# Where the operands of the down-projection pieces stand in ScalarE's queue, in both feed-forwards of a fused encoder block

## The chip, the core and the metric

The kernel runs on one core of a Trainium2 chip. A core has five engines with a queue each: TensorE (PE in the profile, its weight loads PEld), VectorE (DVE), ScalarE (ACT), GpSimd (POOL) and SyncE (SP). SP and POOL only issue DMAs here. An engine takes its instructions in the order of its queue. The metric is device time in microseconds (us), the median of several runs.

## The reference

One layer of a streaming encoder on 256 tokens of width 2048, all in float32:

```python
def swiglu(h, w_up, w_down):
    gate, up = jnp.split(h @ w_up, 2, axis=-1)
    return (jax.nn.silu(gate) * up) @ w_down

x = x + 0.5 * swiglu(rms_norm(x, ffn1_norm), ffn1_w_up, ffn1_w_down)
...   # gated recurrences (HGRN2 and RG-LRU), then cross-attention: "the middle" below
x = x + 0.5 * swiglu(rms_norm(x, ffn2_norm), ffn2_w_up, ffn2_w_down)
return rms_norm(x, final_norm)
```

Only the two feed-forwards are touched. Their hidden width is 5632, so `w_up` is 2048 x 11264 and `w_down` 5632 x 2048.

## The kernel before

**Precision.** Float32 operands are split in two: a high part `h`, rounded to the matmul's input type, and a low part `l = raw - h`. A product a·b is made of three matmuls: a_h·b_h, a_l·b_h (lines L547, L548) and a_h·b_l (L550). `split` makes both parts of a weight tile: ACT writes `h` (L138), then DVE writes `l` (L139).

**Pieces.** Weights come in pieces of 128 x 2048 (1 MB) that are loaded (`raw`), split and used once. `plan` lists all pieces in the order of their use; `weights` keeps two of them prepared ahead, by calling `prepare`. There are three kinds that matter here:

- *fast* up pieces: the matrix product of a 2x2 block with seven block products in place of eight. Beside the weights (512 columns by 4, of which 3 are split as `h`, `l`, 1536 columns) they need four sums of them, `td`, 2048 columns. In the first feed-forward (ffn1) DVE makes the sums, L285 the first two, L287 and L288 one each; in the second (ffn2) some come ready from DRAM (loaded at L277; they were made during the middle). The sums are split in two halves of 1024 columns into `th` and `tl`: the last four lines of `prepare`. The second half (called the *second high part* below) needs L287 and L288, and PE uses it last.
- *plain* down pieces: one load (L270), one `split` of 2048 columns.
- *added* down pieces: ACT writes `l = -raw` (L254), a POOL DMA adds the weights to that from DRAM (L255), and ACT writes `h` later (L263). Their load is L253.

**Groups.** The hidden width is worked off in 11 groups of 512. From the fourth group on a group is eight up pieces (seven or eight of them fast), then four down pieces of earlier groups, here D1, D2, D3 and D4 in the order of use. D1, D2 and D3 are plain, D4 is added. D1 follows the last fast piece of its group. While the down pieces run, the group's seven sums in PSUM are turned into gate and up: L634 on ACT, L635, L636, L643, L646 on DVE, the SiLU at L580 on ACT (twice) and the product at L581 on DVE (twice). Transposes on PE (L588) and `hidop` (L592, L593) follow, and D4's products after the transposes. L662 adds a finished down result to the residual. In ffn1 these values are named `ev`, in ffn2 `hid` and `hd`.

**What sets the order.** A scheduler orders each engine's queue by its own estimate of times; only data dependences, buffers and hints bind it. Such a hint is `tc.issue_after(ins)`: every instruction traced inside is queued behind `ins` on the engine of `ins`; it adds no wait by itself. Buffers that matter: three `raw`, three `h`, three `l`; ffn2 has two `raw2` tiles more. A `raw` tile is free for its next load when the last split that reads it has run.

Of the kernel before, what the change touches and what calls it, by code (L numbers as in the profile page):

```python
# [77 lines left out]
def block_kernel(ctx: ExitStack, tc: tile.TileContext, xT, xin, memT, vec, gfin, bgate, lruw, wu1, wd1, win, wv,  # L78
# [55 lines left out]
    done = {}  # L134


    def split(h, l, raw):
        done["high"] = act.activation(h, raw, ACT.Copy).ins  # L138
        done["low"] = dve.tensor_tensor(out=l, in0=raw, in1=h.bitcast(F32), op=ALU.subtract).ins  # L139

    def split_tiles():
        return hp.tile([P, 2048], F32R, name="h", tag="h"), lp.tile([P, 2048], F32R, name="l", tag="l")


    plan, ahead, made_ahead = [], [], []
# [60 lines left out]
    def beside(i):  # L206

        if under_way and (i >= under_way[0][0] or "prep" not in scoped):
            next(under_way.pop(0)[1])
        if made_ahead and "prep" in scoped and i >= turn[0] and i < first_second - 4:  # L210
            turn[0] = i + (3 + len(made_ahead) % 2 if "scores" in scoped else 3 if len(made_ahead) % 3 else 2)
            steps = make_ahead(*made_ahead.pop(0))
            next(steps)
            under_way.append((i + (2 if "scores" in scoped else 3), steps))
# [5 lines left out]
    def weights(*key):  # L220
        while plan and len(ahead) < 2:
            i = next(planned)
            k, src, kind = plan.pop(0)
            if i == 0:
                in_turn.enter_context(tc.manual_schedule(engines={sp.engine, act.engine, dve.engine}))
            if i < len(head):
                head[i]()
            if plan and plan[0][2] == "added":
                begun.append(begin_added(plan[0][1]))
            ahead.append((k, prepare(src, kind, 4 if i < 4 else 1)))  # L230
            if i in rest:
                rest[i]()
            beside(i)
            if i == 7:
                in_turn.close()
        k, w = ahead.pop(0)
        assert k == key, (k, key)
        return w
# [4 lines left out]
    def raw_tile():  # L243

        if "raw2" in scoped and next(loads) % 5 > 2:
            return scoped["raw2"].tile([P, 2048], F32, name="raw2", tag="raw2")
        return rawp.tile([P, 2048], F32, name="raw", tag="raw")

    def begin_added(src):

        raw = raw_tile()
        l = lp.tile([P, 2048], F32R, name="l", tag="l")
        sp.dma_start(raw, src)  # L253
        act.activation(l, raw, ACT.Copy, scale=-1.0)  # L254
        nc.gpsimd.dma_start(l, src, accum_op=ALU.add)  # L255
        return raw, l

    def prepare(src, kind, cuts=1):

        if kind == "added":  # L260
            raw, l = begun.pop(0)
            h = hp.tile([P, 2048], F32R, name="h", tag="h")
            done["high"] = act.activation(h, raw, ACT.Copy).ins  # L263
            return h, l
        raw = raw_tile()
        n = 2048 // cuts
        if kind == "plain":
            h, l = split_tiles()
            for a in range(0, 2048, n):
                sp.dma_start(raw[:, a:a + n], src[:, a:a + n])  # L270
                split(h[:, a:a + n], l[:, a:a + n], raw[:, a:a + n])
            return h, l
        if kind == "ready":
            src, t = src
            sp.dma_start(raw[:, 512:], src[:, 512:])
            td = raw_tile()
            sp.dma_start(td, t)  # L277
        else:
            sp.dma_start(raw, src)
            if "raw2" in scoped:  # L280
                td = raw_tile()
            else:
                td = scoped["wide"].tile([P, 2048], F32, name="td", tag="wide")
            two = [v[:, a:a + 1024].rearrange("p (i n) -> p i n", i=2) for v, a in ((td, 0), (raw, 512))]
            dve.tensor_tensor(out=two[0], in0=raw[:, None, :512].broadcast_to([P, 2, 512]), in1=two[1],  # L285
                              op=ALU.subtract)
            dve.tensor_tensor(out=td[:, 1024:1536], in0=raw[:, 1024:1536], in1=td[:, :512], op=ALU.subtract)  # L287
            dve.tensor_tensor(out=td[:, 1536:], in0=raw[:, 1536:], in1=td[:, 1024:1536], op=ALU.subtract)  # L288
        h, l = split_tiles()
        if kind != "fast added":  # L290
            split(h[:, 512:], l[:, 512:], raw[:, 512:])
        else:
            act.activation(l[:, 512:], raw[:, 512:], ACT.Copy, scale=-1.0)
            nc.gpsimd.dma_start(l[:, 512:], src[:, 512:], accum_op=ALU.add)
            done["high"] = act.activation(h[:, 512:], raw[:, 512:], ACT.Copy).ins
        th = hp.tile([P, 2048], F32R, name="h", tag="h")
        if "wide" in scoped:
            tl = scoped["wide"].tile([P, 2048], F32R, name="tl", tag="wide")
        else:
            tl = lp.tile([P, 2048], F32R, name="tl", tag="l")  # L300
        for a in (0, 1024):
            split(th[:, a:a + 1024], tl[:, a:a + 1024], td[:, a:a + 1024])
        return (h, l), (th, tl)

    def product(xs, *ws, late=()):
# [19 lines left out]
    def two_ahead(xs, name, i, at, late=()):  # L325

        if i == at:
            both = product(xs, weights(name, i), weights(name, i + 1), late=late)
            two_ahead.next = both[1]
            return both[0]  # L330
        return two_ahead.next if i == at + 1 else product(xs, weights(name, i))[0]
# [233 lines left out]
    def ffn(name, pairs, sq, then, begin=(), sums=()):  # L565
# [37 lines left out]

        for at, e in enumerate(order):
            w = weights(name, *e)
            kind = e[0]
            following = order[at + 1][0] if at + 1 < len(order) else None
# [708 lines left out]
```

## Time and profile before

| | |
|---|---|
| median of 3 runs | 2424.43 us (2424.29, 2424.43, 2427.4) |
| the profiled execution | 2427.28 us, of which the span from first to last instruction is 2425.5 us |
| mean granted TensorE clock | 0.998 |
| engines busy | PE 99%, DVE 84%, ACT 60%, POOL 4% |
| feed-forwards | ffn1 from the start to about 702 us; ffn2 from about 1739 us to the end |

In a row of the timeline stand the start, the duration, the engine, the line, the operation, what it writes and reads, and how many instructions are merged; in brackets the idle time of that engine ahead of it and what ended it. A matmul over 512 columns has a duration of 0.39 us in such rows, but they are pipelined: four in a row take 1.07 us, so one starts every 0.227 us.

### The profile page before, as it was taken

What the parts mean: (1) busy time and instruction counts of PE and PEld (TensorE: products, weight loads), DVE (VectorE), ACT (ScalarE), POOL (GpSimd) and SP (SyncE); (2) the same over time, 40 slices, a digit from 0 to 9 for tenths busy, and PEclk for the clock granted to TensorE, in tenths of its full rate; (3) what the DMA queues carried; (4) which work ended last, traced back from release to release, by engine and by line L of the source; (5) the groups of instructions that cost most, each with busy time, mean ns of one, the idle gap of its engine ahead of it and who ended that gap; (6) DMA issues with size and microseconds to landing.
All of it is one profiled execution on the core that took longest, in us unless ns stands there. A gap on an engine that the chain in (4) does not pass through costs nothing.

```text
span 2425.5 us, 30763 instructions
## 1 busy us (share of the span) xinstructions
PE 2409.3 (99%) x12139; PEld 2013.6 (83%) x12139; DVE 2025.6 (84%) x2260; ACT 1455.0 (60%) x1485; POOL 102.2 (4%) x166
## 2 busy tenths in 40 slices
PE   9999999999999999999999999999999999999998
PEld 8888888888788888888888888888888788888887
DVE  7999999998876868779776788777789999999995
ACT  8567677777664454476434555445676666666664
POOL 0000000000000000000000000000000000000000
PEclk9999999999999999999999999999999999999999
DMA  7579999988858776778989889977798878787873
GB/s 294 195 229 287 272 272 270 275 269 268 266 183 323 268 289 241 294 289 323 346 313 349 310 332 354 335 272 263 264 343 308 285 266 293 273 286 276 294 273 144
DMA packets 102385, 684.31 MB, mean 282 GB/s; under 512 B 11361, under 2 KB 11617, under 8 KB 29281
## 3 DMA queue, kind: packets, MB, share of 16 engines
q1 hardware_dynamic: 78192, 518.68, 57.5%
q0 software_dynamic: 23328, 162.54, 22.4%
q8 instruction: 95, 1.56, 0.2%
q10 hardware_dynamic: 720, 1.13, 0.1%
q14 instruction: 50, 0.40, 0.0%
HBM read 619.39 MB, written 62.91 MB: 281 GB/s over the span
## 4 chain that ended last, share of the span: by engine, by line
PE 91%; DVE 3%; DMA 3%; ACT 1%; issue 1%; ACTq 0%; DVEq 0%; SPq 0%
PE acc L547 16%; PE acc L548 16%; PE acc L550 16%; PE acc L313 11%; PE acc L338 8%; PE acc L341 8%; PE acc L339 8%; PE acc L316 6%; DMA raw<-wd 2%; DVE tl L139 1%; ACT h L138 1%; DVE l L139 1%; PE acc L588 1%; PE acc L477 1%; DMA t<-prep 0%
## 5 line engine op out<-in xcount | busy, mean ns | idle before, releaser
L138 ACT ACTIVATE h<-raw 128x2048 fp32r<-128x2048 f32 (+3 forms) x578 | 870.5, 1531 | 620.2 <-PE acc L339 189.6
L139 DVE TENSOR_TENSOR l<-raw,h 128x2048 fp32r<-128x2048 f32 (+2 forms) x406 | 837.3, 2065 | 187.6 <-ACT h L138 186.1
L547 PE MATMUL acc<-h,xh 128*128 128x512 f32 x1241 | 485.2, 392 | 2.7 <-ACT h L138 2.4
L548 PE MATMUL acc<-h,xl 128*128 128x512 f32 x1241 | 483.0, 390 | 0.0
L338 PE MATMUL acc<-h,ops 128*128 128x512 f32 x832 | 326.8, 393 | 0.0
L339 PE MATMUL acc<-h,ops 128*128 128x512 f32 x832 | 324.5, 390 | 0.0
L547 PEld LDWEIGHTS acc<-h,xh 128*128 128x128 f32 x1241 | 233.3, 188 | 56.2 <-ACT h L138 8.0
L547 PE MATMUL acc<-h,hidop 128*128 128x512 f32 x704 | 276.5, 393 | 2.3 <-ACT h L138 2.2
L313 PE MATMUL acc<-ops,h 128*128 128x512 f32 x1152 | 278.2, 393 | 0.0
L548 PE MATMUL acc<-h,hidop 128*128 128x512 f32 x704 | 274.8, 390 | 0.0
L548 PEld LDWEIGHTS acc<-h,xl 128*128 128x128 f32 x1241 | 233.3, 188 | 47.5
L313 PEld LDWEIGHTS acc<-ops,h 128*128 128x128 f32 x1152 | 211.7, 188 | 41.6
L139 DVE TENSOR_TENSOR tl<-raw,h 128x1024 fp32r<-128x1024 f32 x172 | 203.7, 1220 | 14.9 <-ACT h L138 14.5
L341 PE MATMUL acc<-l,ops 128*128 128x512 f32 x832 | 205.8, 389 | 0.0
L550 PE MATMUL acc<-l,hidop 128*128 128x512 f32 x704 | 189.3, 389 | 0.0
L138 ACT ACTIVATE h<-td 128x1024 fp32r<-128x1024 f32 x126 | 131.3, 1057 | 92.9 <-PE acc L548 42.3
L341 PEld LDWEIGHTS acc<-l,ops 128*128 128x128 f32 x832 | 156.2, 188 | 32.4
L338 PEld LDWEIGHTS acc<-h,ops 128*128 128x128 f32 x832 | 156.2, 188 | 32.2
L339 PEld LDWEIGHTS acc<-h,ops 128*128 128x128 f32 x832 | 156.3, 188 | 31.5
L139 DVE TENSOR_TENSOR tl<-td,h 128x1024 fp32r<-128x1024 f32 x126 | 152.0, 1220 | 31.2 <-ACT h L138 31.0
L200 DVE TENSOR_TENSOR prep<-prep 128x512 f32<-128x512 f32 x232 | 159.7, 689 | 20.9 <-DMA prep<-wu 17.1
L550 PE MATMUL acc<-l,xh 128*128 128x512 f32 x645 | 176.4, 389 | 0.0
(242 smaller groups left out, 2739.4 us busy)
## 6 DMA issues: line engine op xcount, KB each, us to landing
raw<-wu SPq DMA_DIRECT2D x114, 1024.0 KB, 6.3
raw<-wd SPq DMA_DIRECT2D x88, 1024.0 KB, 6.3
prep<-wu POOLq DMA_DIRECT2D x58, 1024.0 KB, 7.8
t<-prep POOLq DMA_DIRECT2D x58, 1024.0 KB, 7.8
raw<-t SPq DMA_DIRECT2D x58, 1024.0 KB, 6.9
raw<-wu SPq DMA_DIRECT2D x58, 768.0 KB, 5.0
raw<-win SPq DMA_DIRECT2D x40, 1024.0 KB, 4.8
raw<-wg SPq DMA_DIRECT2D x32, 1024.0 KB, 6.1
```

What stands on the lines that cost most here:

```text
L138: done["high"] = act.activation(h, raw, ACT.Copy).ins
L139: done["low"] = dve.tensor_tensor(out=l, in0=raw, in1=h.bitcast(F32), op=ALU.subtract).ins
L200: dve.tensor_tensor(out=b[o], in0=b[x], in1=b[y], op=ALU.subtract)
L313: pe.matmul(acc, h[:, k * P:(k + 1) * P], xs[k], start=k == 0, stop=False)
L316: done["product"] = pe.matmul(acc[:, :T], l[:, k * P:(k + 1) * P], xs[k][:, :T], start=False, stop=k == KT - 1).ins
L338: pe.matmul(accs[t], x[:, t * P:][:, :P], h[j], start=first and j == 0, stop=False)
L339: pe.matmul(accs[t], x[:, T + t * P:][:, :P], h[j], start=False, stop=False)
L341: done["product"] = pe.matmul(accs[t], x[:, t * P:][:, :P], l[j], start=False, stop=last and j == 3).ins
L477: pe.transpose(acc[:, z * T + t * P:][:, :P], tile[:, t * 512 + (2 * y + z) * P:][:, :P], ident)
L547: pe.matmul(acc, ah, bh, start=start, stop=False)
L548: pe.matmul(acc, al, bh, start=False, stop=False)
L550: pe.matmul(acc, ah, bl, start=False, stop=stop)
```

## The change

`prepare` learns whether a piece is a down piece. The two operations of a plain down piece's split are traced inside `issue_after(done["sums"])`, where `done["sums"]` is the last ACT instruction of the sums of the latest fast piece: its second high part. So ACT's write of a plain down piece's `h` is queued behind the second high part of the fast piece in front. Added pieces return earlier and are not touched, nor is any DMA's line. For D2 and D3 the same `ins` holds.

```diff
-            ahead.append((k, prepare(src, kind, 4 if i < 4 else 1)))
+            ahead.append((k, prepare(src, kind, 4 if i < 4 else 1, k[1] == "down")))
...
-    def prepare(src, kind, cuts=1):
+    def prepare(src, kind, cuts=1, down=False):
...
                 sp.dma_start(raw[:, a:a + n], src[:, a:a + n])
-                split(h[:, a:a + n], l[:, a:a + n], raw[:, a:a + n])
+                with tc.issue_after(done["sums"]) if down else ExitStack():
+                    split(h[:, a:a + n], l[:, a:a + n], raw[:, a:a + n])
...
         for a in (0, 1024):
             split(th[:, a:a + 1024], tl[:, a:a + 1024], td[:, a:a + 1024])
+        done["sums"] = done["high"]
```

The lines below the first edit in `prepare` move by one or two: L285 becomes L286, L634 becomes L636; L254 and L263 keep their numbers. The text names lines by their numbers before. What the scheduler makes of it is shown at three places. First, ACT's queue at the end of a group of ffn1 (the one whose down pieces start at about 630 us). `h_4375<-td` is a half of the last fast piece's sums, `h_4400` is D1's high part, `h_4443` D2's, `l_4475` the first step of D4. Before:

```order
L138 ACTIVATE h_4375<-td_4367 128x1024
L138 ACTIVATE h_4400<-raw_4399 128x2048
L138 ACTIVATE h_4375<-td_4367 128x1024
L138 ACTIVATE h_4443<-raw_4442 128x2048
L634 ACTIVATE ev_4429<-acc_4156 128x512
L254 ACTIVATE l_4475<-raw_4474 128x2048
```

After:

```order
L138 ACTIVATE h_4375<-td_4367 128x1024 x2
L138 ACTIVATE h_4400<-raw_4399 128x2048
L138 ACTIVATE h_4443<-raw_4442 128x2048
L636 ACTIVATE ev_4429<-acc_4156 128x512
L254 ACTIVATE l_4475<-raw_4474 128x2048
```

D1's high part moves from ahead of the second high part to behind it. The same happens in the other groups from the fourth on, in ffn1 and in ffn2.

Second, ACT's queue in the fourth group of ffn2, whose down pieces start at about 1920 us. `h_15436<-raw2` are the halves of the sums, `h_15464` is D1's high part, `h_15505` D2's, `h_15542` D3's; `l_15537` is D4's first step (L254) and `h_15573` D4's high part. Before:

```order
L138 ACTIVATE h_15436<-raw2_15428 128x1024
L634 ACTIVATE hid_15490<-acc_15203 128x512
L138 ACTIVATE h_15464<-raw2_15463 128x2048
L138 ACTIVATE h_15436<-raw2_15428 128x1024
L138 ACTIVATE h_15505<-raw_15504 128x2048
L254 ACTIVATE l_15537<-raw_15536 128x2048
L138 ACTIVATE h_15542<-raw_15541 128x2048
L263 ACTIVATE h_15573<-raw_15536 128x2048
L580 ACTIVATE hid_15490<-hid_15490,rtok_14335 128x512 x2
```

After:

```order
L138 ACTIVATE h_15436<-raw2_15428 128x1024
L636 ACTIVATE hid_15490<-acc_15203 128x512
L138 ACTIVATE h_15436<-raw2_15428 128x1024
L138 ACTIVATE h_15464<-raw2_15463 128x2048
L138 ACTIVATE h_15505<-raw_15504 128x2048
L138 ACTIVATE h_15542<-raw_15541 128x2048
L582 ACTIVATE hid_15490<-hid_15490,rtok_14335 128x512 x2
L263 ACTIVATE h_15573<-raw_15536 128x2048
L254 ACTIVATE l_15537<-raw_15536 128x2048
```

Here D4's first step has moved as well: it stood third behind D1's high part, now it stands behind D3's, both SiLUs and D4's own high part. In the other groups of ffn2 and in ffn1 it keeps its place behind D2's high part.

Third, DVE's queue at the same place. `tl_15437` are the low parts of the sums, `l_15465` is D1's low part, `l_15506` D2's, `l_15543` D3's; rows with `hd` and `hid` belong to gate and up. Before:

```order
L139 TENSOR_TENSOR l_15465<-raw2_15463,h_15464 128x2048
L139 TENSOR_TENSOR tl_15437<-raw2_15428,h_15436 128x1024
L139 TENSOR_TENSOR l_15506<-raw_15504,h_15505 128x2048
L635 TENSOR_TENSOR hd_15491<-acc_15208,hid_15490 128x512
L636 TENSOR_TENSOR hd_15491<-acc_15207,hd_15491 128x512
```

After:

```order
L139 TENSOR_TENSOR tl_15437<-raw2_15428,h_15436 128x1024
L637 TENSOR_TENSOR hd_15491<-acc_15208,hid_15490 128x512
L139 TENSOR_TENSOR l_15465<-raw2_15463,h_15464 128x2048
L638 TENSOR_TENSOR hd_15491<-acc_15207,hd_15491 128x512
```

D1's low part moves behind the second half of `tl` and one step of gate and up; D2's low part, which stood third, now follows the whole chain of gate and up, just ahead of D3's. PE's queue changes with it in ffn2: before, the first products of D1 stood ahead of those of the second high part; now they stand behind them. SP's and POOL's queues keep their order.

## The prediction

> **What bounds the kernel.** I read the page's totals first, then the table of waits for PE, then the timelines of PE, ACT, DVE and POOL around the longest of those waits.
>
> ```profile
> span 2425.5 us, 30763 instructions
> PE 2409.3 (99%) x12139; PEld 2013.6 (83%) x12139; DVE 2025.6 (84%) x2260; ACT 1455.0 (60%) x1485; POOL 102.2 (4%) x166
> ```
> ```profile
> PE acc L547 <- ACT h L138: 4.6, 5, 2.0
> ...
> PE acc L550 <- DVE tl L139: 0.4, 1, 0.4
> ```
>
> PE is the bound: it is busy for 2409.3 of 2425.5 us, and the second view (total us, number, longest) gives it 4.6 us of waiting for high parts and 0.4 us for low parts. No reordering on ACT can win much more than these 5 us and what they drag behind them; it can lose without a limit, since nothing hides a PE wait. 0.2% of the median, about what a measurement of this kernel can tell from no change, is 4.85 us, so the sum decides by small terms.
>
> Two of the five waits make up most of the 4.6 us. The largest is in the fourth group of ffn2. PE:
>
> ```profile
> 1917.64 0.73 PE L550 MATMUL acc<-tl,xh 128*128 128x512 f32 x2 [0.37 <-DVE tl L139]
> 1920.41 0.50 PE L547 MATMUL acc<-h,hidop 128*128 128x512 f32 x1 [2.04 <-ACT h L138]
> ```
>
> ACT there (D1, the second high part and D2 are merged in the first row), then DVE, then POOL's issue of D4's accumulating DMA with the landing times of the eight such DMAs in ffn2:
>
> ```profile
> 1918.45 4.66 ACT L138 ACTIVATE h<-raw 128x2048 fp32r<-128x2048 f32 x3 [1.00 <-DMA raw<-wd]
> 1923.01 1.90 ACT L254 ACTIVATE l<-raw 128x2048 fp32r<-128x2048 f32 x1
> 1924.81 1.90 ACT L138 ACTIVATE h<-raw 128x2048 fp32r<-128x2048 f32 x1
> 1928.27 1.92 ACT L263 ACTIVATE h<-raw 128x2048 fp32r<-128x2048 f32 x1 [1.55 <-PE acc L548]
> 1930.10 1.31 ACT L580 ACTIVATE hid<-hid,rtok 128x512 f32<-128x512 f32 x2
> ```
> ```profile
> 1917.50 0.69 DVE L288 TENSOR_TENSOR raw<-raw,raw 128x512 f32<-128x512 f32 x1
> 1920.39 2.29 DVE L139 TENSOR_TENSOR l<-raw,h 128x2048 fp32r<-128x2048 f32 x1 [2.20 <-ACT h L138]
> 1922.60 1.22 DVE L139 TENSOR_TENSOR tl<-raw,h 128x1024 fp32r<-128x1024 f32 x1
> ...
> 1926.93 0.69 DVE L636 TENSOR_TENSOR hd<-acc,hd 128x512 f32<-128x512 f32 x1
> ...
> 1928.74 0.68 DVE L646 TENSOR_TENSOR hid<-acc,hd 128x512 f32<-128x512 f32 x1
> ...
> 1930.83 1.42 DVE L581 SCALAR_TENSOR_TENSOR hid<-hd,rtok,hid 128x512 f32<-128x512 f32 x2 [0.22 <-ACT hid L580]
> ```
> ```profile
> 1925.34 0.88 POOL L255 DMA_DIRECT2D l<-wd  x1 [213.99 <-ACT l L254]
> ```
> ```profile
> DMA to landing us min/median/max: 11.8/12.9/13.9
> ```
>
> ACT stood idle for D1's load, in front of a second high part whose sums were complete when L288 ended, at 1918.19. PE waited 2.04 us, and the windows behind it show the price of that: the granted clock (seventh value of the row, after the five busy times) was half for 3.4 us.
>
> ```profile
> 1921.40:1924.80 3.40, 3.40 (x9) 2.65 (x9) 3.40 (x3) 3.40 (x2) 0.00 (x0) 0.50 0.63 193
> ```
>
> The other long wait is in ffn1, of the same make (PE, ACT, DVE):
>
> ```profile
> 628.53 0.50 PE L547 MATMUL acc<-h,xh 128*128 128x512 f32 x1 [1.66 <-ACT h L138]
> ```
> ```profile
> 625.62 1.92 ACT L138 ACTIVATE h<-raw 128x2048 fp32r<-128x2048 f32 x1 [2.25 <-DMA raw<-wd]
> 627.44 1.04 ACT L138 ACTIVATE h<-td 128x1024 fp32r<-128x1024 f32 x1
> ```
> ```profile
> 625.52 0.69 DVE L288 TENSOR_TENSOR td<-raw,td 128x512 f32<-128x512 f32 x1
> ```
>
> **The change, part by part.** No instruction is added or removed. I sum against the profiled execution, 2427.28 us; it lies 2.85 us above the median, to which I come back.
>
> *ffn1, the wait at 628.* The second high part no longer stands behind D1. It starts when L288 ends, 626.21, takes 1.04 us and ends at 627.3 in place of 628.48: **-1.2 us**. The rest is still DVE's. Of the other three waits for high parts (4.6 - 2.04 - 1.66, 0.9 us) I take **-0.5 us**, between nothing and all, because in the usual group of ffn1 DVE sets the second high part and not D1:
>
> ```profile
> 314.45 1.93 ACT L138 ACTIVATE h<-raw 128x2048 fp32r<-128x2048 f32 x1 [0.53 <-PE acc L548]
> 316.79 1.06 ACT L138 ACTIVATE h<-td 128x1024 fp32r<-128x1024 f32 x1 [0.41 <-DVE td L288]
> ```
>
> Here D1 was done at 316.38, ACT was idle, and the second high part came at L288's end. Behind the change it comes at the same time, and D1 only after it, at 317.8: 3.4 us later.
>
> *What D1's delay pushes in ffn1.* D1's low part (2.29 us behind a high part that ends at 319.7) ends at 322.0 in place of 318.95, and D3's load goes into D1's buffer:
>
> ```profile
> 318.98 0.33 SPq L270 DMA_DIRECT2D raw<-wd  x1
> ```
> ```profile
> raw<-wd SPq DMA_DIRECT2D x1, 1024.0 KB, 5.3
> ```
> ```profile
> 333.68 0.84 PE L550 MATMUL acc<-l,hidop 128*128 128x512 f32 x3
> ```
>
> Issued at 322.0 and landing 5.3 us later (the second row), it gives D3's high part from 327.3 to 329.2; the second SiLU and its product (halves of 1.31 and 1.42 us, from the rows of L580 and L581 above) end at 330.6, D3's low part at 332.9. PE asks for it at 333.68 (third row). So 0.75 us of cover is left where the load takes 5.3 us, and each us beyond 6.0 is a us of PE's, in six groups. I take **+0.5 us**, ends 0 and +6 (a load of 7.0). Of the DMA streams the Trainium skill says, in "DMA: Bandwidth & Descriptors", section "Issuing engines are not separate DMA queues", that transfers of SyncE and GpSimd run on the same engines and interleave; that speaks against this change, since the later load meets D4's transfer. The trace agrees: D1's load at 613.72, in flight with a GpSimd transfer, took 11.8 us.
>
> ```profile
> raw<-wd SPq DMA_DIRECT2D x1, 1024.0 KB, 11.8
> l<-wu POOLq DMA_DIRECT2D x1, 768.0 KB, 12.2
> ```
>
> *ffn2, fourth group.* The second high part runs from 1918.24 to 1919.3, D1's to 1921.1, D2's to 1923.0, D3's to between 1924.9 and 1926.7 (its load was in by 1924.81 at the latest). PE does the products of the second high part first and reaches D1 at 1921.2, not later than it may: 72 matmuls of D1 to D3 at 0.227 us, and then, as before, from D3's last low products to D4's first,
>
> ```profile
> 1938.95 1.07 PE L550 MATMUL acc<-l,hidop 128*128 128x512 f32 x4
> ...
> 1942.59 1.07 PE L550 MATMUL acc<-l,hidop 128*128 128x512 f32 x4
> ```
>
> 3.64 us, bring it to D4's low part at 1921.2 + 68 x 0.227 + 3.64, **1940.3**, 2.3 us sooner than now. But that low part is not there. Its first step, L254, now follows both SiLUs and D4's high part. The SiLUs wait for gate and up on DVE: the second `tl` ends at 1920.5, one step and D1's low part bring DVE to 1924.2, and from L636 to the end of L646 are 2.5 us, 1926.7. So the SiLUs end at 1927.4 to 1928.0, D4's high part at 1929.3 to 1929.9, L254 at 1931.2 to 1931.8. POOL issues 0.43 us behind that, as it does now (1924.91 to 1925.34), and 11.8 to 13.9 us on the data lands: 1943.4 to 1946.1, middle **1944.7**. PE waits about 4.4 us and starts D4's low products 2.1 us later than before: **+2.1 us** (0.8 to 3.5). A wait this long halves the clock for a window, as 2.04 us did: **+1.7 us** (0 to 1.7; the half window of today is inside the 1942.59). The Trainium skill ("TensorE: Matmul & The Clock Gate", section "HAM oscillation — how this bites in real kernels") asks for no idle gap over about 3.4 us. This trace differs, since 2.04 us with 0.37 us ahead of it sufficed; by the page a wait of 3.1 us, that of the earliest landing, would leave the 1.7 us out and the sum at +1.6 us.
>
> *The other seven groups of ffn2.* Here L254 stays behind D2.
>
> ```profile
> 2042.00 0.69 DVE L288 TENSOR_TENSOR raw<-raw,raw 128x512 f32<-128x512 f32 x1
> ```
> ```profile
> 2047.22 0.62 PE L550 MATMUL acc<-l,hidop 128*128 128x512 f32 x2
> ```
>
> From L288's end at 2042.69 the second high part (1.05), D1's high part (1.92) and low part (2.29) follow each other with some 0.05 us of handing over, to 2048.0. PE comes to that low part three matmuls later than now, at 2047.9. A wait of 0.1 us, seven times: **+0.7 us** (-0.5 to +2).
>
> The sum is -1.2 - 0.5 + 0.5 + 2.1 + 1.7 + 0.7 = +3.3 us, 2430.6 us against 2427.28. One of the three unprofiled runs, 2427.4, is like the profiled one; two are near 2424.3. If these two lack the late load and the half clock at 1920 (2.04 and 1.7 us, about their 2.85), the changed kernel loses that head start in the new wait, whose end hangs on L288 and not on D1's load, and stays at 2430.6. If the 2.85 us lie elsewhere it comes to 2427.7. I take 2429.5, nearer the first.
>
> **The rivals.** *D4's data is in time* (not slower). If L254 runs some 4 us earlier than I work out, or the transfer takes under 8.5 us, the fourth group gains 2.3 us in place of losing 3.8, and the sum is -2.8: 2424.5, or 2421.6 from the median. It decides at 1940.3 us. For it: the two waits that go are real, and with the three small ones and the half clock all of them are worth up to 7 us, 2417.5 from the median. Against it: no transfer of the eight in ffn2 was under 11.8 us. I give it 0.24, 0.10 of that beyond 0.2% faster.
>
> *Loads in ffn1 become the bound* (slower). D3's load, three us later, meets D4's transfer and takes 7.0 us in place of 5.3: six waits of 1.0 us, 2436. For it is the load of 11.8 us; against it that most of it is through before POOL's transfer begins, about 324. 0.14.
>
> *Nothing moves* I exclude, as the queues differ in sixteen groups.
>
> **How the numbers follow.** The forecast's case has 0.62: 0.34 of it over 2429.3 and 0.28 below, by where the 2.85 us lie. With the rivals: slower 0.34 + 0.14 = 0.48; same 0.28 + 0.14 = 0.42; faster 0.10. The case's own range is 2425.5 (all low ends together, -1.8 us) to 2434 (the high ends of D4's wait and of the later groups, without the second rival). For 8 in 10 I go from 2420.5, most of the first rival, to 2435, most of the second.
>
> **What would show it.** In the changed kernel's profile: at 628 a PE wait of about 0.5 in place of 1.66 us; in the fourth group of ffn2 no wait of 2.04 us for D1, but one of some 4 us of PE on the low part that the DMA `l<-wd` fills, with that DMA issued near 1932 and the clock at half behind it; D1's low part about 0.1 us late in the later groups. I am wrong if PE enters D4's low products there by 1942, or if PE's waits in ffn1 grow beyond 2 us.

## The result, and the profile after

The changed kernel takes 2438.65 us (median of 2433.55, 2436.93, 2440.38 and 2440.46) against 2425.91 us for the kernel before on the same chip: a ratio of 1.0046, 95% interval 1.0031 to 1.0061. It is slower by 0.46%, 12.7 us, and lies outside the predicted range. The profiled execution is the fastest of the four, 2433.55 us, 6.3 us above that of before; so the trace shows about half of the loss, and the experiments have to tell where the rest is.

First PE's waits in the changed kernel (in total, number, longest). 4.6 and 0.4 us were there before:

```profile
span 2431.4 us, 30788 instructions
```
```profile
PE acc L552 <- DVE tl L139: 5.5, 3, 3.1
PE acc L549 <- ACT h L138: 2.6, 5, 1.0
PE acc L552 <- DMA l<-wd: 2.5, 1, 2.5
```

The waits for high parts have shrunk to 2.6 us: the long ones at 628 and 1920 are gone (0.96 us is left of the second), and three of about 0.5 us are new, at 443, 509 and 572. Beside them stand a wait for D4's data in ffn2, which was forecast, and two long ones on `tl`, 1.96 us at 420 and 3.14 us at 486, which were not. These two are in ffn1, neither on a down piece nor near one: they fall among the fast pieces of the *next* group. PE, DVE, SP's queue and POOL around the longer one:

```profile
485.67 0.73 PE L552 MATMUL acc<-tl,xh 128*128 128x512 f32 x2 [3.14 <-DVE tl L139]
```
```profile
477.28 1.22 DVE L139 TENSOR_TENSOR tl<-td,h 128x1024 fp32r<-128x1024 f32 x1
483.25 1.23 DVE L286 TENSOR_TENSOR td<-raw 128x1024 f32<-128x1024 f32 x1 [4.75 <-DMA raw<-wu]
484.39 1.22 DVE L139 TENSOR_TENSOR tl<-td,h 128x1024 fp32r<-128x1024 f32 x1
```
```profile
472.06 0.33 SPq L280 DMA_DIRECT2D raw<-wu  x1
```
```profile
DMA to landing us min/median/max: 11.1/11.1/11.1
```
```profile
466.39 0.86 POOL L295 DMA_DIRECT2D l<-wu  x1 [15.86 <-ACT l L294]
471.84 0.87 POOL L295 DMA_DIRECT2D l<-wu  x1 [4.58 <-ACT l L294]
```

A load issued at 472.06 lands 11.1 us later. DVE's queue holds the next piece's first sums (L286), which need that load, ahead of the second half of `tl` of the piece in front, which PE needs (the kernel before has the same order there): so DVE stands idle for 4.75 us and PE for 3.14. It is an in-order queue that turns a late load into a wait for something else. The same load of the kernel before, its issue and its landing:

```profile
468.09 0.33 SPq L279 DMA_DIRECT2D raw<-wu  x1
```
```profile
DMA to landing us min/median/max: 6.7/6.7/6.7
```

Two things went together. First, the load was issued late. Equal transposes (L588) of this group run at 460.86 in the kernel before and at 462.89 in the changed one, so PE is 2.03 us behind there; the load is 3.97 us behind. It went out when the last of the sums that read its buffer had run, which is L288 in the kernel before and L289 in the changed one:

```profile
467.34 0.69 DVE L288 TENSOR_TENSOR td<-raw,td 128x512 f32<-128x512 f32 x1
```
```profile
471.31 0.68 DVE L289 TENSOR_TENSOR td<-raw,td 128x512 f32<-128x512 f32 x1
```

Second, being late, it ran beside an accumulating transfer of POOL's: the load of the kernel before was issued 1.72 us ahead of that transfer, this one 0.22 us behind it. The transfer itself (the second row) is not early: it is 2.03 us later than before, like PE.

```profile
464.95 0.87 POOL L294 DMA_DIRECT2D l<-wu  x1 [16.04 <-DVE hidop L593]
469.81 0.86 POOL L294 DMA_DIRECT2D l<-wu  x1 [3.99 <-ACT l L293]
```

From 474 to 481 us the two share the DMA engines, the software queue (POOL's) at 50.9% and the hardware queue (SyncE's) at 38.1%:

```profile
q0 software_dynamic: 117, 0.72, 50.9%
q1 hardware_dynamic: 116, 0.93, 38.1%
```

The order of issue alone doesn't decide. In the same trace a load at 345.43, 0.13 us ahead of a transfer, took 6.7 us, and in the kernel before one at 360.33, 0.04 us behind a transfer, 6.9.

The delay begins further ahead, with the load right behind D3's, that of the first fast piece of the next group. In the kernel before it was issued 1.0 to 2.2 us ahead of D4's transfer in the six groups and took 4.8 to 6.2 us. In the changed kernel it is issued 0.06 us behind that transfer in all six, and takes 7.5 to 10.6. Before:

```profile
445.83 0.33 SPq L279 DMA_DIRECT2D raw<-wu  x1
```
```profile
448.03 0.87 POOL L255 DMA_DIRECT2D l<-wd  x1 [19.97 <-ACT l L254]
```
```profile
DMA to landing us min/median/max: 5.6/5.6/5.6
```

After, with the step of ACT's that waits for the load:

```profile
449.67 0.87 POOL L255 DMA_DIRECT2D l<-wd  x1 [19.55 <-ACT l L254]
```
```profile
449.72 0.33 SPq L280 DMA_DIRECT2D raw<-wu  x1
```
```profile
DMA to landing us min/median/max: 10.6/10.6/10.6
```
```profile
460.38 1.49 ACT L138 ACTIVATE h<-raw 128x1536 fp32r<-128x1536 f32 x1 [2.50 <-DMA raw<-wu]
```

Two differences may stand behind the lost time. The one is the late start of D3's load and of the load behind it; the prediction had the first of the two. The other it had overlooked: in six groups of ffn1 ACT's queue differs at the head of the next group too. The first step of the second fast piece (L294, which starts POOL's transfer) has moved ahead of the `hidop` copies and of the second high part of the first. (It is the transfer at 466.39, about 0.6 us sooner by PE's time. DVE's queue moves with it: the second piece's first sums stand ahead of the second half of the first's `tl`.) Before:

```
ACTIVATE h_2733<-td_2725 128x1024 x2
ACTIVATE hidop_2712<-acc_2707 128x2x256
ACTIVATE hidop_2720<-acc_2715 128x2x256
ACTIVATE l_2772<-raw_2765 128x1536
```

After:

```
ACTIVATE h_2733<-td_2725 128x1024
ACTIVATE l_2772<-raw_2765 128x1536
ACTIVATE hidop_2712<-acc_2707 128x2x256
ACTIVATE hidop_2720<-acc_2715 128x2x256
ACTIVATE h_2733<-td_2725 128x1024
```

And one row of the windows says how little room there was. The kernel before, over 10 us behind D3's load and over a whole group of ffn1; the second last value is the share of the DMA engines that is busy:

```profile
320.00:330.00 10.00, 10.00 (x46) 8.29 (x45) 9.81 (x12) 7.29 (x6) 0.86 (x1) 1.00 0.99 320
310.00:371.80 61.80, 61.66 (x277) 50.83 (x276) 56.45 (x58) 44.09 (x37) 4.35 (x5) 1.00 0.90 272
```

The changed kernel in the same 10 us:

```profile
320.00:330.00 10.00, 10.00 (x45) 8.28 (x45) 9.61 (x12) 7.52 (x7) 0.87 (x1) 1.00 0.76 239
```

The DMA engines are 0.90 busy in a group, next to PE's 1.00. While D3's load waits for D1's buffer they stand idle, 0.76 in place of 0.99 over 10 us, so the loads behind have less of a lead.

The fourth group of ffn2 went much as forecast (ACT, POOL, PE, and the granted clock behind the wait, 0.50). These times are 3.95 us later than in the kernel before, by which the changed kernel is behind when ffn2 begins (the difference between equal evictions in the two traces):

```profile
1932.83 1.90 ACT L254 ACTIVATE l<-raw 128x2048 fp32r<-128x2048 f32 x1
```
```profile
1935.16 0.88 POOL L255 DMA_DIRECT2D l<-wd  x1 [219.87 <-DVE l L139]
```
```profile
1946.89 1.19 PE L552 MATMUL acc<-l,hidop 128*128 128x512 f32 x4 [2.46 <-DMA l<-wd]
```
```profile
1948.50:1951.00 2.50, 2.50 (x7) 1.97 (x6) 1.60 (x3) 0.00 (x0) 0.00 (x0) 0.50 1.04 436
```

### The profile page after: what moved, and what is told of

Same layout as the page of the kernel before. It is cut to its first block, busy times and chain, and to the rows that moved or that the text cites. A ratio compares the mean times of both kernels' runs of the same rounds, so it can differ in the third digit from the quotient of the medians.

```text
span 2431.4 us, 30788 instructions
## 1 busy us (share of the span) xinstructions
PE 2410.6 (99%) x12139; PEld 2012.3 (83%) x12139; DVE 2026.3 (83%) x2260; ACT 1453.3 (60%) x1485; POOL 102.2 (4%) x166
## 4 chain that ended last, share of the span: by engine, by line
PE 92%; DVE 3%; DMA 2%; issue 1%; ACT 1%; DVEq 0%; ACTq 0%; SPq 0%
PE acc L552 17%; PE acc L549 17%; PE acc L550 17%; PE acc L315 11%; PE acc L340 8%; PE acc L343 8%; PE acc L341 8%; PE acc L318 6%; DVE tl L139 1%; DMA raw<-wu 1%; DVE l L139 1%; PE acc L590 1%; PE acc L479 1%; ACT h L138 1%; DMA l<-wd 0%
```

## The experiments

The theory: in ffn1 the DMA engines are nearly full, loads come just in time, and the change takes some of their lead away (late buffer) and lets POOL's transfers run beside them (early transfer); ffn2 adds a little through D4. The rivals: the loss lies in ffn2's fourth group; or D1's new place costs by itself, on ACT and DVE. All medians below stand against the kernel before on the same chip, 2425.85, 2425.74 and 2425.44 us in the three series (23, 30 and 35 runs).

**Which feed-forward.** The flag given for one feed-forward only:

```diff
-prepare(src, kind, 4 if i < 4 else 1, k[1] == "down")
+prepare(src, kind, 4 if i < 4 else 1, k[:2] == ("ffn1", "down"))   # or "ffn2"
```

> The change in the first feed-forward alone. Theory (early start of an accumulating transfer: in five groups of ffn1 the fast-added piece's step L294 moved ahead of the hidop copies and of the second high part of the piece in front, so that POOL's transfer L295 starts 0.7 to 1.4 us sooner, fills the DMA engines, and the next raw<-wu load lands late and stalls DVE, behind which the second half of tl stands): this kernel carries most of the loss, 2431 to 2437 us, with PE waits of 2 to 3 us on tl in one to three groups of ffn1. Rival (the fourth group of ffn2, as the prediction had it): within 1 us of the kernel before, since the -1.7 us at 628 is all that ffn1 does.

> The change in the second feed-forward alone. Theory: +1 to +4 us against the kernel before (the trace of the changed kernel shows +2.0 us over ffn2: 2.0 us of PE waits gone, a wait of 2.5 us for D4's data and a half clock window come in their place), and ffn1 without any PE wait on tl. Rival (the fourth group carries the loss): +8 us or more.

ffn1 alone: 2435.57 us, ratio 1.0040 (1.0029 to 1.0052), +9.7 us. ffn2 alone: 2428.26 us, ratio 1.0006 (0.9997 to 1.0015), +2.4 us. Most of the loss is ffn1's. The profiled execution of ffn1 alone, its fastest (2429.66 us), has a wait on `tl` of 2.23 us at 358 and one of 0.78. ffn2's +2.4 us is about half of the +4.5 that the prediction summed for it (2.1 + 1.7 + 0.7), and its interval takes in zero.

**The changed kernel once more**, unedited, for a second profile:

> The changed kernel once more, for a second profile and for times beside the other kernels of this call: 2434 to 2441 us. Theory: PE waits on tl in ffn1 again, in the same or in other groups, each behind a raw<-wu load of more than 10 us; the more of them, the longer the run. Rival: waits in ffn1 at other places, on D3's low part.

2440.53 us, ratio 1.0056 (1.0042 to 1.0069). Its profiled execution, 2444.28 us, is the slowest of its six. PE's waits, and one of the causes on DVE and in SP's and POOL's queues:

```profile
PE acc L552 <- DVE tl L139: 6.7, 3, 3.2
PE acc L552 <- DMA l<-wd: 3.0, 1, 3.0
PE acc L894 <- DVE k L914: 2.7, 1, 2.7
```
```profile
357.88 1.23 DVE L286 TENSOR_TENSOR td<-raw 128x1024 f32<-128x1024 f32 x1 [4.84 <-DMA raw<-wu]
```
```profile
346.33 16.47 SPq L280 DMA_DIRECT2D raw<-wu  x3
```
```profile
346.38 0.88 POOL L295 DMA_DIRECT2D l<-wu  x1 [4.42 <-ACT l L294]
```

The same chain, but in an earlier group: here load and transfer are issued within 0.05 us of each other, and the load lands 11.5 us later. Which groups are hit differs from one execution to the next, and with it the time. (The wait at L894 is in the middle, which no kernel here changes; it is up to 4.0 us in the profiles of this case, and part of the spread of every kernel.)

**The early transfer taken away.** The changed kernel, with L294 of a group's second fast piece queued behind the second high part of its first:

```diff
-            act.activation(l[:, 512:], raw[:, 512:], ACT.Copy, scale=-1.0)
+            with tc.issue_after(done["sums"]) if second else ExitStack():
+                act.activation(l[:, 512:], raw[:, 512:], ACT.Copy, scale=-1.0)
```

> The whole change, but the step L294 of the second fast piece of a group (the first fast-added one) is queued on ACT behind the second high part of the piece in front, so that POOL's transfer cannot start sooner than before; D1's delay stays. Theory: the PE waits on tl at about 418 and 482 go, the loads of raw<-wu there take 6 to 8 us again, and the time falls by 4 to 8 us against the changed kernel, to 2427 to 2432 us. Rival (D1's delay itself, which makes all later loads of a group late): no change, 2434 to 2441 us.

2432.34 us, ratio 1.0024 (1.0016 to 1.0033): 8.2 us under the changed kernel of the same series, where 4 to 8 were expected. But the waits have not gone. Its profiled execution, the slowest of its twelve, has one of 2.81 us at 359 and one of 3.42 us at 488 (on the same piece as the wait at 486 above):

```profile
PE acc L553 <- DVE tl L139: 6.6, 3, 3.4
PE acc L895 <- DVE k L915: 3.2, 1, 3.2
PE acc L553 <- DMA l<-wd: 2.2, 1, 2.2
```

So the early order makes late loads more frequent or longer, and is not the whole cause. Which part of it does so is not shown: the edit puts DVE's queue at the head of the group back as well.

**The early transfer alone**, put into the kernel before; D1 and D3's load stay where they were:

```diff
+            first = act.activation(l[:, 512:], raw[:, 512:], ACT.Copy, scale=-1.0).ins
+            if second:   # the second high part of the first fast piece goes behind it
+                tc.add_manual_dep(done["sums"], first.name, ...)
```

> The kernel before, with the other suspected cost of the change alone: in every group of ffn1 the first step L293 of the second fast piece stands ahead of the hidop copies and of the second high part of the piece in front, as in the changed kernel; D1, and with it the load of D3, stays where it was. If the early transfer costs by itself: +4 to +7 us against the kernel before (the difference between ffn1 alone, +9.7, and the kept order, +6.5 less ffn2's 2.4), with raw<-wu loads of over 10 us behind it. If it costs only behind late loads: within 1.5 us of the kernel before.

2426.81 us, ratio 0.9999 (0.9988 to 1.0010), and no PE wait on `tl` over 0.4 us. By itself the early order, which DVE's queue shows here too, costs nothing that can be seen.

**The late buffer alone**, put into the kernel before. A tiny DVE step behind D2's low part reads D1's buffer once more:

```diff
+            if k[0] == "ffn1" and len(downs) == 2 and all(e[0][1] == "down" for e in plan[:2]):
+                with tc.issue_after(done["low"]):
+                    dve.tensor_tensor(out=spare, in0=downs[0][:, :8], in1=downs[0][:, :8], op=ALU.subtract)
```

> The kernel before, with one suspected cost of the change alone: in ffn1 a 128x8 step on DVE behind D2's low part reads D1's raw tile once more, so that its buffer comes free some 3.4 us later and D3's load starts about 322.2 in place of 318.98, as in the changed kernel. POOL's transfers start where they did. Theory (the DMA engines are 0.90 busy over a group of ffn1; what stands idle at 319 to 322 is paid back by late raw<-wu loads in the next pieces): +3 to +8 us against the kernel before, PE waits on tl at one or two of 358, 420, 484, and loads of raw<-wu of over 10 us in front of them. Rival (only the early start of POOL's transfer counts): within 1.5 us of the kernel before.

2433.72 us, ratio 1.0036 (1.0022 to 1.0050): +8.0 us, with D1 itself in its old place, where D3's load is issued 2.75 us later than in the trace of before (about 3.6 by PE's time; 3.0 in the changed kernel). It goes out as D2's low part ends, at 321.71, and the load behind it, at 322.40, as the added step ends. That second load takes 9.6 to 11.0 us in the six groups, slow as in the changed kernel. D3's load and the share of the DMA engines behind it:

```profile
321.73 0.33 SPq L276 DMA_DIRECT2D raw<-wd  x1
```
```profile
320.00:330.00 10.00, 10.00 (x46) 8.26 (x45) 8.81 (x13) 6.76 (x5) 0.86 (x1) 1.00 0.71 229
```

The idle DMA engines of the changed kernel are there again, 0.71. The profiled execution is this kernel's fastest (2426.68 us; the others reach 2440.84) and shows no long wait on `tl`, 0.53 us at 357 at most, so the waits expected at 358, 420 and 484 were not seen. Even so it loses 3.3 us to the trace of before between equal transposes at 337 and 523; that the late buffer costs +8.0 rests on the times. The step moved D3's high part behind the second SiLU, and one step of DVE's per group, as well, so the edit isn't pure.

**Room for the DMA engines.** The accumulating transfers of ffn1's fast-added pieces are left out, from the kernel before and from the change in ffn1 alone, so the low part of these pieces is missing from the product. The steps on ACT and the other queues stay:

```diff
-            nc.gpsimd.dma_start(l[:, 512:], src[:, 512:], accum_op=ALU.add)
```

> The kernel before without the accumulating transfers of the fast-added pieces of ffn1 (their low part is left at minus the weights, so this part of the product is not computed): a baseline in which the DMA engines have room, some 0.7 busy in place of 0.90 over a group of ffn1. Both theories: 2421 to 2427 us, PE waits in ffn1 not over those of the kernel before.

> The change in ffn1 alone, likewise without the accumulating transfers of the fast-added pieces, to stand beside the kernel before without them. Theory (full DMA engines): the loss of ffn1 is gone, between -2 and +1 us against that kernel, no PE wait on tl over 0.5 us. Rival (D1's delay or the order on ACT and DVE costs by itself, without the transfers): +5 us or more, as with the transfers (+9.7).

Before without them: 2424.27 us; the change in ffn1 without them: 2423.92 us, ratios to the kernel before 0.9995 (0.9987 to 1.0004) and 0.9992 (0.9983 to 1.0002). The group of the change in ffn1, without the transfers:

```profile
310.00:371.80 61.80, 61.76 (x277) 50.91 (x276) 56.67 (x58) 44.04 (x38) 0.87 (x1) 1.00 0.66 222
```

With the DMA engines at 0.66 the same order of instructions costs nothing: -0.35 us where it cost +9.7. The rival that D1's place costs by itself, on ACT or DVE, has fallen. The load behind D3's still runs beside D4's transfer here and takes 7.7 to 11.6 us; what follows makes it good (the load in the place of the one at 345.43 lands in 4.7 us). The run doesn't separate the room from the collisions: it takes away both the load on the engines and the transfers that loads run beside.

**More lead for the loads.** A fourth `raw` buffer in ffn1, under the changed kernel and under the kernel before:

```diff
-    FFN1_POOLS = dict(wide=3, hd=1, xd=2)
+    FFN1_POOLS = dict(wide=3, xd=2, raw4=1)
...
+        if "raw4" in scoped and next(fourth) % 4 == 3:
+            return scoped["raw4"].tile([P, 2048], F32, name="raw4", tag="raw4")
```

> The changed kernel with a fourth raw buffer in ffn1 (room for it by giving the scratch of the sums of squares a place in another pool), so that D3's load no longer waits for D1's split. Theory: DMA share between 320 and 330 back over 0.9, the waits on tl gone, 2425 to 2430 us (what is left is ffn2's +2.4 us). Rival (D1's place in the queues costs by itself): still over 2434 us.

> The kernel before with the same fourth raw buffer, as the baseline of the kernel above: theory 2421 to 2426 us, since loads can only start sooner; the wait at 628 shorter than 1.66 us because D1's load no longer meets the transfer so late.

Changed: 2427.82 us, ratio 1.0005 (0.9994 to 1.0016). Before: 2425.06 us, ratio 0.9997 (0.9986 to 1.0008). The loss of ffn1 is gone; what is left of the change is 2.8 us, about ffn2's share. PE's waits and the window:

```profile
PE acc L554 <- DMA l<-wd: 2.4, 1, 2.4
PE acc L551 <- ACT h L138: 1.1, 2, 1.0
...
PE acc L554 <- DVE tl L139: 0.4, 1, 0.4
```
```profile
320.00:330.00 10.00, 10.00 (x45) 8.28 (x45) 9.96 (x12) 7.74 (x7) 0.88 (x1) 1.00 0.78 247
```

One expectation was wrong: the share between 320 and 330 did not come back, it is 0.78. With four buffers D3's load is issued at 315.87, and it is the next load that waits for D1's low part, until 321.06. The engines stand idle there as before, but each load has a piece more of lead. So a low share in a window is no cost in itself. What counts is how far ahead of their use the loads run.

**ffn2 with D4's first step put back** ahead of the SiLUs, of D3's and of D4's high part, in the fourth group only:

```diff
+        for silu in done.get("silus", []):   # the two SiLUs of that group
+            tc.add_manual_dep(silu, first.name, ...)
+        if done.pop("silus", []):
+            done["sums"] = done["D4"] = first   # D3's split and D4's high part go behind it
```

> The change in ffn2 alone, with D4's first step L254 in the fourth group put back ahead of the SiLUs, of D3's and of D4's high part, so that POOL's transfer starts about 1925.3 and not 1930.3. Theory (the fourth group as in the prediction: that wait and its half clock are what ffn2 loses): no wait on l<-wd there, no half clock behind it, 2422 to 2425 us against 2428.3 for ffn2 alone. Rival (D1's later low part in the other seven groups): no change against ffn2 alone.

2425.17 us, ratio 1.0000 (0.9992 to 1.0009), 3.1 us under ffn2 alone, though the two intervals overlap. In its trace the wait on `l<-wd` and the half clock behind it are gone, and 0.3 us on a low part of DVE's is left in their place; that ffn2's loss was D4's late data, as the prediction had it, rests on both. The expected gain below the kernel before is too small to see in the medians. The profiled executions show it: between the evictions at 1877 and 1997 the pinned kernel takes 1.85 us less than the kernel before, and 0.38 us more from there on.

**The change in two groups only**, where the trace of before has its two long waits (the last of ffn1, and the fourth of ffn2 pinned as above):

```diff
-k[:2] == ("ffn2", "down")
+k[1] == "down" and last[0] in (("ffn1", NG - 1), ("ffn2", 3))
```

> The change only where the trace of before has its two long waits: in the last group of ffn1 (the wait at 628) and in the fourth group of ffn2, there with D4's first step put back ahead of the SiLUs as in the pinned kernel. No other group's queue changes. Theory: 2420.5 to 2423.5 us, 2 to 5 us under the kernel before: the waits of 1.66 and 2.04 us and the half clock go, and nothing is delayed that the full DMA engines of ffn1 would have to make good. Rival (each wait is made good later in any case): 2425 to 2427 us.

2424.70 us, ratio 0.9996 (0.9986 to 1.0007). The two waits are gone from its trace (0.96 us is left of the second), but -0.7 us is no gain that can be told from none; the 2 to 5 us expected were wrong. One reason shows: the wait of 1.66 us at 628 is a matter of the execution. With that place unchanged it is there in two profiles (before, and ffn2 alone with 1.5 us) and missing in two (ffn2 pinned, and the early transfer). A wait of the same make stands in another group instead, 1.39 us at 258 in ffn2 pinned and 1.53 us at 258 here. The wait at 1920 is no such matter: all seven profiles with ffn2 unchanged have it, 1.87 to 2.04 us.

## Why the prediction was wrong, step by step

- *The wait at 628, -1.2 us.* Gone altogether in the changed kernel's profile. The step held; its worth did not, since two of the four profiles that leave this place alone don't have that wait.
- *The three small waits, -0.5 us.* Not as forecast. Of the three, which stood at 256 (0.53 us), 1915 and 1983 (0.19 each), only that at 1915 stayed, and the waits at 443, 509 and 572, 1.5 us in sum, are new.
- *D1's delay in ffn1, +0.5 us.* **Here the prediction failed.** D3's load was issued at 321.29 (322.0 forecast) and PE never waited for D3, as worked out; the load took 4.7 to 5.9 us. But the step ended at D3. It asked whether that one load comes in time and not what the loads behind it lose: the next one ran beside D4's transfer and took 7.5 to 10.6 us, and the pieces after it started late. The row of DMA shares, 0.90 over the group and 0.99 behind D3's load, was the hint that a lead once lost is slowly regained. By ffn1 alone the term measures about +10 to +11 us (+9.7, and the gain at 628 back) in place of +0.5, the early order included; the late buffer alone gave +8.0. The prediction's own sign of being wrong came true: PE's waits in ffn1 grew to 6.6 us, where it allowed 2.
- *The other queues' order.* The prediction showed the tail of a group and took it that the rest stands. L294's new place in six groups, and DVE's order with it, was not seen. It costs nothing by itself (ratio 0.9999); together with the late buffer, taking it away won 8.2 us.
- *The fourth group of ffn2, +3.8 us.* By the times of the trace of before POOL issued at 1931.2, 0.4 us ahead of the forecast 1931.6 to 1932.2; the data landed at 1942.9, just under the 1943.4 forecast as earliest; PE waited 2.46 us, not 4.4, and the half clock followed. Between equal evictions at 1877 and 1997 the profiled loss is 1.65 us. Right in mechanism, some 2 us too large.
- *The other seven groups, +0.7 us.* From there to the end the changed kernel loses 0.35 us more.
- *The choice between 2430.6 and 2427.7.* It hung on whether the two faster runs of the kernel before lack the late load at 1920. That they lack it is not borne out: the wait there is in all seven profiles with ffn2 unchanged, the half clock behind it in five. By that step's own condition the sum would have been 2427.7, further from what was measured.
- *The rivals.* "Loads in ffn1 become the bound" was nearest, in engine and time (2436), with a chance of 0.14. Its place was wrong by one load: D4's transfer did not slow D3's load but the `raw<-wu` load behind it, and then `l<-wu` transfers slowed loads of later pieces. "D4's data is in time" did not happen.

Not settled is how the loss in ffn1 divides: the late buffer alone gives +8.0 us, the change with the early transfer taken away +6.5 with ffn2's 2.4 in it. Their intervals overlap. The early order's own part lies between nothing and these 8.2 us. Nor does any run say why a load beside a transfer takes 6 us in one place and 11 in another.

## What to carry to other kernels

Before a load is moved later, read the share of the DMA engines over the whole stage, not only whether that load still lands in time: at 0.90, three us lost on one load of each group came back as 8 us in all, and at 0.66, with the transfers beside the loads gone, as none. Follow a reordering past the place that it edits, to where the next buffers and the other queues' transfers start. And a wait seen in one profile is worth only what it is in most executions.

## What the runs showed of the hardware

An accumulating transfer costs the DMA engines about twice as much per byte as a load. The kernel before, 400 to 422 us (packets, MB, share of the 16 engines; the hardware queue is SyncE's, the software queue GpSimd's):

```profile
q1 hardware_dynamic: 468, 3.43, 41.9%
q0 software_dynamic: 288, 1.57, 40.2%
```

That is 40.2% of 22 us for two transfers of 768 KB, 4.4 us of all engines each, and 2.8 us for a load of 1 MB. Leaving four of them out of a group agrees: (0.90 - 0.64) x 61.8 / 4 = 4.0 us each, with the group of the kernel before without them:

```profile
310.00:371.80 61.80, 61.76 (x277) 50.92 (x276) 56.44 (x58) 44.19 (x37) 0.87 (x1) 1.00 0.64 222
```

The Trainium skill ("DMA: Bandwidth & Descriptors", section "Issuing engines are not separate DMA queues") says that transfers started by SyncE and by GpSimd run on the same engines and interleave; the trace agrees, with 50.9% and 38.1% for the two queues while the load of 11.1 us was under way.

A wait of 2 to 3 us halves the clock sometimes and sometimes not. Behind the 3.14 us at 485.67 in the changed kernel's first profile the granted clock stayed at 1.00; behind 3.23 us, at 360.30 in its second, it was 0.57 over 3.5 us:

```profile
485.50:489.50 4.00, 3.83 (x17) 3.16 (x18) 4.00 (x4) 2.56 (x2) 0.48 (x1) 1.00 0.26 33
```
```profile
361.00:364.50 3.50, 3.50 (x11) 2.74 (x10) 3.50 (x3) 1.88 (x2) 0.78 (x1) 0.57 0.24 61
```

Length does not sort them either. Behind 3.42 us, at 487.85 in the changed kernel with the early transfer taken away, the clock stayed at 1.00 (first row); behind 1.87 us, at 1919.97 in the kernel with the late buffer alone, it was half (second row).

```profile
486.00:495.00 9.00, 7.15 (x31) 5.93 (x32) 9.00 (x8) 5.58 (x5) 0.89 (x1) 1.00 0.47 136
```
```profile
1920.90:1924.20 3.30, 3.30 (x10) 2.56 (x9) 3.30 (x3) 3.30 (x2) 0.00 (x0) 0.50 0.63 217
```
